# Half the memory tokens in activation places, the first key weight ahead of the memory, GDN ratios scaled on VectorE, and another order and other banks for the down projection

## The chip, the cores and the metric

The kernel runs on one core of a Trainium2 chip. The metric is the device time of one execution in microseconds; the profile that goes with it is one execution taken by the hardware profiler. A core has TensorE (matrix products, with a separate path for loading weights), VectorE, ScalarE, GpSimd and SyncE; each works through its own instructions in order, and waits on semaphores where it needs another engine's result. Transfers are issued on queues; this kernel issues nearly all of them from SyncE (SP), a few from ScalarE and VectorE.

## The reference

One layer of a hybrid encoder for 512 tokens of width 2048, with 256 memory tokens:

```python
h = x
y = rmsnorm(h, norm_mix) @ w_in                  # 7520 columns
h = h + concat[GDN(y_gdn), RWKV7(y_rwkv)] @ w_out
hn, mn = rmsnorm(h, norm_xattn), rmsnorm(mem, norm_mem)
q, k, v = hn @ wq, mn @ wk, mn @ wv              # 4 heads of 512
h = h + softmax(q k^T / sqrt(512)) v @ wo
hn = rmsnorm(h, norm_mlp)
h = h + square(relu(hn @ w_up)) @ w_down         # hidden 8192
out = rmsnorm(h, norm_final)
```

GDN is a gated delta rule with 8 heads of 128, RWKV7 a recurrence with 16 heads of 64. In chunks, both need the inverse of a unit lower triangular matrix for every head and chunk:

```python
M = where(strict, einsum(kb, kc) * gamma, 0)     # kb = k * beta, gamma = exp(G_i - G_j)
sol = triangular_solve(M + I, rhs)               # unit diagonal
```

All arithmetic is in 32 bits.

## The kernel before, in words

**Products.** A 32-bit operand is split into two parts of a reduced 32-bit type, `hi` (ScalarE copies it into that type) and `lo` (VectorE subtracts `hi` from the original). A product is then `hi hi + lo hi + hi lo`. For the 256 memory tokens a tile `mhl` of 512 columns holds `hi` in its left half and `lo` in its right, so one key weight block costs one product of 512 columns with the weight's `hi` and one of 256 with its `lo` (lines 594 to 603 of the listing below, in `projections`).

**Stages.** The program runs through these, with TensorE nearly always busy:

1. Input projection: 59 output blocks of 128 columns (`py0` to `py58`), each with a weight of 2048 x 128 in two halves of 512 KB. Meanwhile the heads of both recurrences are worked on as soon as their columns are there (`rwkv`, `gdn`); their small products stand between the large ones. The profile has the end of the last projection product at about 911 us.
2. Memory keys (`kp0` to `kp15`): 16 output blocks, each in two halves of 8 products with `hi` and 8 with `lo`. The first two blocks are worked on half by half: `kpo` gives (0,0), (1,0), (0,1), (1,1), then one block after the other. The last heads of the recurrences go on beside this.
3. Query weights times keys (`kq`), which starts only after the inverse of the last GDN head ("inverted", 7).
4. Attention, values and output, the recurrence's output product, written in plain order.
5. The MLP, up and then down, by a scheme of seven products on 2 x 2 blocks in place of eight: sums of blocks (`s1` to `s4` of the weights, `T1` to `T4` of the activations) are multiplied with each other, and every product is added to one or several output blocks. Names: `B11`, `B21`, `B22` are products of plain activation blocks, `T1` to `T4` those of sums. A unit is one (e, g) part of up or down; the units are a list, down has ten.

**What sets the order.** In stages 1 to 3, and again in stage 5, the program is written as generators (`chain(generator, rank)`) that yield one instruction at a time. A planner at build time (`run`, with `start`, `cost` and `issue`) keeps a clock for every engine and a landing time for every tile, and issues at each step the chain whose next instruction can start first; ranks break ties. A generator can also yield a condition (`after("x", 4)`, or a lambda), and is passed over until that holds. So the order on every engine follows from durations that the planner believes, and an edit in one chain moves instructions of others. A lane such as `SL` or `SM` is an engine or a queue with an extra wait or margin that the planner adds for its transfers.

**The weights' ring.** All weights of stages 1 to 3 come through a ring of raw tiles (`wraw`), in the order of the list `wq`; each entry is loaded when an earlier one has been split. Entries of kind "s" are memory tokens for the sum of squares, of kind "m" memory tokens for the keys (four k-blocks of 128 features each, 512 KB), of kind "w" weight halves. For "m", `memory` splits four k-blocks with the gain `norm_mem` into `mhl` tiles. These take the places of the activation tiles `xhi`, `xlo` of the projection, which share 32 buffers (tag "act"): `after("x", i)` holds when the last projection block `py58` is through with k-blocks up to i. The end of `wq` is: memory 0, 1, 2, first key weight half, memory 3, the other key weights.

**The inverses.** `inverse_blocks` writes the matrices to memory on SP, reads 16 x 16 diagonal blocks back in a layout for GpSimd, inverts them there, and writes and reads the result (tiles `bg..T`, `bg..U`); `inverse_levels` builds the 64 x 64 inverses from them on TensorE, with copies by VectorE. For GDN, the matrix is `NTm = pkk * Es`, with `pkk` the products of keys in the PSUM bank `pkk` and `Es = E * sneg`, E the ratios exp(G_i - G_j) and `sneg` the negative strict mask.

**Down's banks.** A unit of down works with three pairs of PSUM banks: `mm` for B21, `mg` for T1 and B22, and for the rest `scr` and `scg` in units of odd number, or two `mx` in units of even number (`odd` in `multiply_`). A product that adds to a bank which an earlier one of the same unit has used waits until VectorE has added that one into h ("snap" events, set in `downout`). The order of the seven products is given by `order_of`, with one order for the very last unit.

Nearly every instruction of stages 1 to 3 and 5 is issued at one line of `issue`, so the profile shows it as L256: the name of the tile tells what it is.

## Time and profile before

| what | us |
|---|---|
| median of 3 runs | 2902.29 |
| lowest and highest | 2901.53, 2903.21 |
| profiled execution | 2902.95 |
| its span, from first to last instruction | 2901.2 |

The profiled execution took 1.75 us more than its span. Its mean granted clock of TensorE is 0.999 of full speed.

A row of the timeline is a start in us, a length, the engine, the line of the kernel, the operation, output tile <- input tiles with partitions x elements, and the number of instructions joined in that row; in brackets stand the idle time before it on that engine and what ended it. PE is TensorE, PEld its weight load, DVE VectorE, ACT ScalarE, POOL GpSimd, SP SyncE; a q behind the name (SPq, ACTq) means the engine's queue of transfers, where a row's length is the issue's and not the transfer's. Buffer numbers are left out of names, so `kp` stands for all of `kp0` to `kp15`. Where several matrix products are joined, the last one's end includes its way through the array; the step between two is better read from the starts.

### The profile page before, as it was taken

How to read it: one execution, taken by the hardware profiler on the slowest of the kernel's cores; microseconds unless marked ns; L12 is line 12 of the kernel's file. 1: busy time of each engine (PE TensorE's matmuls, PEld its weight loads, DVE VectorE, ACT ScalarE, POOL GpSimd, SP SyncE). 2: the span in 40 equal slices, each digit the busy share in tenths (PEclk: the TensorE clock that was granted, in tenths of full speed). 3: DMA queues.
4: the chain of work that ended last, by engine and by line, in shares of the span. 5: the costliest groups of instructions: out<-in, count | busy, mean ns of one | idle time of the engine just before them, and what ended most of it. 6: DMA issues, size and time to landing. Idle time of an engine off the chain costs nothing.

```text
span 2901.2 us, 49161 instructions
## 1 busy us (share of the span) xinstructions
PE 2868.0 (99%) x18794; PEld 2420.4 (83%) x18794; DVE 2333.1 (80%) x3551; ACT 1569.9 (54%) x2233; POOL 227.0 (8%) x547
## 2 busy tenths in 40 slices
PE   8999999999999999999999999999999999999998
PEld 7877877777777888879988888888888888888887
DVE  7787787787887876769956898899998878787888
ACT  6454555545655555564444656555555645454544
POOL 0213213223122100000000000000000000000000
PEclk9999999999999999999999999999999999999999
DMA  5657556556656688684423344656665878978733
GB/s 190 175 143 184 160 160 173 161 154 185 173 154 198 199 256 276 229 286 159 125 94 94 106 157 158 196 194 203 187 201 181 291 243 278 296 256 273 267 102 109
DMA packets 320924, 553.01 MB, mean 191 GB/s; under 512 B 101096, under 2 KB 188396, under 8 KB 320688
## 3 DMA queue, kind: packets, MB, share of 16 engines
q1 hardware_dynamic: 293296, 518.41, 57.9%
q10 hardware_dynamic: 27392, 31.46, 3.1%
q8 instruction: 147, 2.41, 0.3%
q14 instruction: 89, 0.73, 0.1%
HBM read 443.45 MB, written 106.31 MB: 189 GB/s over the span
## 4 chain that ended last, share of the span: by engine, by line
PE 93%; DMA 2%; DVE 2%; ACT 1%; issue 1%; ACTq 0%; SPq 0%; DVEq 0%
PE py L256 22%; PE mxu L256 12%; PE mgd L256 6%; PE mgu L256 6%; PE mxd L256 6%; PE op L122 5%; PE vp L122 3%; PE mmu L256 3%; PE sc L122 3%; PE at L122 3%; PE mmd L256 3%; PE scrd L256 3%; PE scgd L256 3%; PE kq L256 3%; PE kp L256 3%; PE vo L122 1%
## 5 line engine op out<-in xcount | busy, mean ns | idle before, releaser
L256 ACT CAST whi<-wraw 128x1024 fp32r<-128x1024 f32 (+1 forms) x366 | 383.4, 1048 | 364.2 <-PE py L256 150.4
L256 DVE TENSOR_TENSOR wlo<-wraw,whi 128x1024 fp32r<-128x1024 f32 (+1 forms) x366 | 450.5, 1231 | 101.0 <-ACT whi L256 92.2
L256 PE MATMUL py<-xhi,whi 128*128 128x512 f32 x928 | 372.6, 401 | 8.1 <-ACT xhi L256 8.1
L256 PE MATMUL py<-xhi,wlo 128*128 128x512 f32 x928 | 372.8, 402 | 0.0
L256 PE MATMUL py<-xlo,whi 128*128 128x512 f32 x928 | 372.7, 402 | 0.0
L256 ACT CAST whi<-w 128x1024 fp32r<-128x1024 f32 x176 | 185.3, 1053 | 170.3 <-PE mxd L256 35.2
L256 DVE TENSOR_TENSOR wlo<-w,whi 128x1024 fp32r<-128x1024 f32 x176 | 214.8, 1221 | 44.4 <-ACT whi L256 41.1
L256 PE MATMUL mxu<-cb,whi 128*128 128x512 f32 x1016 | 249.3, 392 | 0.0
L256 PEld LDWEIGHTS mxu<-cb,whi 128*128 128x128 f32 x1016 | 184.7, 189 | 34.3
L256 PEld LDWEIGHTS py<-xhi,whi 128*128 128x128 f32 x928 | 175.0, 189 | 42.6 <-ACT xhi L256 8.1
L256 PEld LDWEIGHTS py<-xhi,wlo 128*128 128x128 f32 x928 | 175.0, 189 | 35.5 <-issue 1.8
L256 PEld LDWEIGHTS py<-xlo,whi 128*128 128x128 f32 x928 | 174.9, 189 | 34.8 <-DVE xlo L256 0.5
L131 DVE TENSOR_TENSOR wlo<-wraw,whi 128x1024 fp32r<-128x1024 f32 x112 | 136.6, 1221 | 44.0 <-ACT whi L130 43.5
L130 ACT CAST whi<-wraw 128x1024 fp32r<-128x1024 f32 x112 | 117.6, 1051 | 85.9 <-PE op L122 29.4
L256 PE MATMUL mxu<-cb,wlo 128*128 128x256 f32 x1016 | 142.7, 283 | 0.7 <-DVE wlo L256 0.7
L256 PEld LDWEIGHTS mxu<-cb,wlo 128*128 128x128 f32 x1016 | 135.1, 191 | 6.0 <-DVE wlo L256 0.9
L256 ACT ACT_TABLE_LOAD x87 | 111.6, 1283 | 36.4 <-DVE suml_gn L256 16.5
L256 PE MATMUL mgu<-cb,whi 128*128 128x512 f32 x512 | 129.3, 394 | 0.1
L256 PE MATMUL mxd<-whi,cb 128*128 128x512 f32 x512 | 126.7, 389 | 0.7 <-DVE acc L256 0.7
L256 PE MATMUL mgd<-whi,cb 128*128 128x512 f32 x512 | 126.4, 389 | 0.0
L256 ACT CAST whi<-ws 128x1024 fp32r<-128x1024 f32 x75 | 79.0, 1053 | 72.3 <-PE mgu L256 48.2
L122 PE MATMUL op<-ob,whi 128*128 128x256 f32 (+1 forms) x752 | 115.3, 304 | 0.1
(945 smaller groups left out, 6447.2 us busy)
## 6 DMA issues: line engine op xcount, KB each, us to landing
wraw<-in_w_in SPq DMA_DIRECT2D x116, 512.0 KB, 4.6
wraw<-in_w_up SPq DMA_DIRECT2D x65, 512.0 KB, 3.6
w<-in_w_up SPq DMA_DIRECT2D x63, 512.0 KB, 4.0
ds<-in_w_dm SPq DMA_DIRECT2D x128, 205.0 KB, 4.1
sd_s<-ds SPq DMA_DIRECT2D x128, 205.0 KB, 4.7
wraw<-sd_s SPq DMA_DIRECT2D x51, 512.0 KB, 4.9
w<-sd_s SPq DMA_DIRECT2D x50, 512.0 KB, 5.5
w<-in_w_dm SPq DMA_DIRECT2D x48, 512.0 KB, 5.0
```

Of the source, the lines that this page charges most:

```text
L122: PE.matmul(o, l, r, start=start, stop=stop, skip_group_check=again)
L130: S.copy(hi, src)
L131: V.tensor_tensor(out=lo, in0=src, in1=hi.bitcast(F32), op=ALU.subtract)
L256: f(*a, **k)
```

## The change

It has four parts.

1. In `wq` the first key weight half stands ahead of the memory entries, and only memory 0 and 1 come through the ring. Memory 2 and 3 are loaded by a new chain, `straight`, in four transfers of 256 KB on SP (lane `SD`: no extra wait, a landing margin of 1500 ns), directly into four of the 32 activation places. For this the 32 buffers are divided into 28 with tag "act" and 4 with tag "acr": `act_tile` puts `xhi4`, `xlo4`, `xhi5`, `xlo5` into the four (`x in (4, 5)`), and afterwards the tiles that come to those places by count. The first two of these loads wait for `after("x", 4)`, the others for `after("x", 5)`. A second new chain, `placed`, splits `mhl8` to `mhl15` from there, after `mhl7` has been begun; `mhl` is a dictionary now.
2. In `gdn` the multiplication `E * sneg` moves from GpSimd, ahead of the key's norm, to VectorE, directly ahead of the multiplication with `pkk`. It occurs once for each of 8 heads.
3. The last unit of down takes T1 second, B22 ahead of T3: B11, T1, T2, B22, T3, B21, T4.
4. `odd` is turned round: in all ten units of down the banks `scr`, `scg` and the two `mx` are exchanged, so the first unit of down uses `scr` and `scg`, the last one `mx`.

Since the planner orders stages 1 to 3 anew, part 1 and 2 move instructions beyond their own. The new lane takes a line above `issue`, so the issue line reads L257 in the changed kernel.

SP's queue around the last RWKV inverse, in the kernel before. `sr<-ndri7` above the first row is the read for GpSimd, `bg16T` and `bg16U` write the inverted blocks, `r` and `E2` read them, `wraw<-in_wk` is a key weight half, `wraw<-in_memT` memory tokens, `ds` and `sd` belong to sums of down's weights that are worked out early.

```order
L256 DMA bg16T_195<-sr_549_10077 64x16x16
L256 DMA bg16U_196<-sr_549_10077 64x16x16
...
L256 DMA r_557_10299<-bg16T_195 64x8x64 x2
L256 DMA E2_558_10300<-bg16U_196 64x4x64 x4
L256 DMA wraw126_10395<-in_wk 128x1024
L256 DMA sd3_1_s1_154<-ds02_55_829 128x410
L256 DMA sd3_1_s3_156<-ds01_54_828 128x410
L256 DMA wraw127_10444<-in_memT 128x1024
L256 DMA sd3_1_s2_155<-ds00_53_827 128x410
L256 DMA wraw128_10475<-in_wk 128x1024
```

And in the changed kernel, first at the read for the inverse, then from `bg16T` on (`mraw` are the four new loads):

```order
L257 DMA sr_549_10099<-ndri7_10094 64x16x16
L257 DMA wraw123_10126<-in_wk 128x1024
L257 DMA wraw124_10175<-in_memT 128x1024
...
L257 DMA bg16T_195<-sr_549_10099 64x16x16
L257 DMA bg16U_196<-sr_549_10099 64x16x16
L257 DMA wraw125_10354<-in_memT 128x1024
L257 DMA r_563_10357<-bg16T_195 64x8x64 x2
L257 DMA E2_564_10358<-bg16U_196 64x4x64 x4
L257 DMA mraw0_10417<-in_memT 128x512
L257 DMA mraw1_10425<-in_memT 128x512
L257 DMA mraw2_10428<-in_memT 128x512
L257 DMA mraw3_10434<-in_memT 128x512
L257 DMA wraw126_10402<-in_wk 128x1024
```

The first key weight (`wraw126` before, `wraw123` now) moved from behind the eight transfers of the inverse to the place right after its read; the second (`wraw128` before, `wraw126` now) stands behind the four `mraw`.

TensorE at the end of the key products, before: `gi7u` is the last product of the last GDN inverse, `TtG` the copy of it by VectorE, `gs2_7_0` the first product that reads that copy.

```order
L256 MATMUL kp13_11636<-mhl15_10571,whi_144_11602 128x512
L256 MATMUL gi7u1_11609<-TtG_194,gkn_591_11560 64x64 x4
L256 MATMUL kp14_11700<-mhl0_10364,whi_145_11638 128x512
L256 MATMUL kp14_11700<-mhl1_10376,whi_145_11638 128x512
...
L256 MATMUL kp14_11700<-mhl7_10439,whi_145_11638 128x512
L256 MATMUL gs2_7_0_11729<-gv_587_11324,TtG_194 128x128
L256 MATMUL kp14_11700<-mhl0_10364,wlo_145_11639 128x256
```

And in the changed kernel:

```order
L257 MATMUL kp15_11762<-mhl14_10572,whi_148_11728 128x512
L257 MATMUL kp15_11762<-mhl15_10620,whi_148_11728 128x512
L257 MATMUL gi7u1_11734<-TtG_194,gkn_591_11682 64x64 x4
L257 MATMUL gs2_7_0_11841<-gv_587_11554,TtG_194 128x128
L257 MATMUL kq0_0_0_11843<-khl0_10660,whi_149_11764 128x512
L257 MATMUL kq0_0_0_11843<-khl1_10715,whi_149_11764 128x512
L257 MATMUL kq0_0_0_11843<-khl2_10849,whi_149_11764 128x512
```

The key products that stood behind `gi7u` stand ahead of it now; `gs2_7_0` follows on `gi7u` directly, and the first query product `kq0` after that.

TensorE in the last unit of down, before: the end of B11 (`wlo_261`) and the start of T2 (`whi_262`). `scr` and `scg` are the banks, `cb` the activations.

```order
L256 MATMUL scgd3_1_0_1_27235<-whi_261_17933,cb0_7_17866 128x512
L256 MATMUL scrd3_1_0_0_27234<-wlo_261_17934,cb0_6_17150 128x512 x2
L256 MATMUL scgd3_1_0_1_27235<-wlo_261_17934,cb0_6_17150 128x512 x2
L256 MATMUL scrd3_1_0_0_27234<-whi_262_17935,cb0_2_17146 128x512
L256 MATMUL scrd3_1_0_0_27234<-whi_262_17935,cb0_3_17147 128x512
```

And in the changed kernel, the end of B11 and the start of what follows it, T1:

```order
L257 MATMUL mxd3_1_0_1_27239<-whi_261_17949,cb0_7_17882 128x512
L257 MATMUL mxd3_1_0_0_27238<-wlo_261_17950,cb0_6_17166 128x512 x2
L257 MATMUL mxd3_1_0_1_27239<-wlo_261_17950,cb0_6_17166 128x512 x2
L257 MATMUL mgd3_1_1_0_27272<-whi_262_17951,cb5_6_17201 128x512
L257 MATMUL mgd3_1_1_0_27272<-whi_262_17951,cb5_7_17887 128x512
```

B11 now fills the `mx` banks, and the product behind it goes to `mg` instead of to the banks that B11 has just filled.

The diff, without its unchanged surroundings where these tell nothing:

```diff
...
                 return self.key, nm, getattr(self.eng, nm), a, k, out, aps, self.slack
             return op
 
+    SD = Lane(nc.sync, "SP", 0.0, 1500.0)
     SL, SM = Lane(nc.sync, "SP", wait=6000.0), Lane(nc.sync, "SP", margin=8000.0)
     DV, AC, GS, TE, SY = (Lane(e, k) for e, k in ((V, "DVE"), (S, "ACT"), (GP, "POOL"), (PE, "PE"), (nc.sync, "SP")))
 
...
         yield TE.matmul(pt, which, hi, start=False, stop=True)
         lock.pop()
 
-    def act_tile(nm, dt=F32R):
-        return tile_of(pa, [P, 512], dt, "act", nm, 32)
+    acts = [0]
+
+    def act_tile(nm, dt=F32R, x=None):
+        few = x in (4, 5)
+        if x is None:
+            few = acts[0] // 4 in (7, 11, 19, 27, 35)
+            acts[0] += 1
+        return tile_of(pa, [P, 512], dt, "acr" if few else "act", nm, 4 if few else 28)
 
     mixd = [pd.tile([P, T], F32, name=f"mixd{i}", tag=f"mixd{i}") for i in range(16)]
     KQd = [pd.tile([P, 1024], F32, name=f"kqd{i}", tag=f"kqd{i}") for i in range(16)]
...
                 yield from presum(e, m, c, min(c + width, 2048), d, Lane(nc.sync, "SP", margin=5000.0), Lane(nc.sync, "SP", 0.0, 0.0))
 
     hk = [("w", I["wk"][n][:, h * 1024:(h + 1) * 1024]) for n, h in kpo]
-    wq += [("m", m) for m in mem4[:3]] + hk[:1] + [("m", mem4[3])] + hk[1:]
+    wq += hk[:1] + [("m", m) for m in mem4[:2]] + hk[1:]
     wq += [("w", I["wqT"][n][:, g * 1024:(g + 1) * 1024]) for n in range(KD) for g in range(2)]
     NKP, NKQ = 2 * NIN, 2 * NIN + 2 * KD
     raws, halves, used, whole, piece = {}, {}, set(), set(), {}
...
                 whole.add(w)
                 w += 1
             else:
-                yield from (memory if kind == "m" else squares)(nm % 4, raws[i])
+                yield from (memory if nm >= 4 else squares)(nm % 4, raws[i])
                 nm += 1
             if NWR < i + NWR <= 2 * NWR:
                 chain(late(i + NWR), 2)
...
 
     def xin():
         for k in range(KD):
-            hi, lo = act_tile(f"xhi{k}"), act_tile(f"xlo{k}")
+            hi, lo = act_tile(f"xhi{k}", x=k), act_tile(f"xlo{k}", x=k)
             yield from split_(xr[k], hi, lo, col("norm_mix", k))
             xhi.append(hi)
             xlo.append(lo)
...
             wh, wl = halves[NKP + i]
             for part in (0, 1) if h == 0 else (1, 0):
                 for k in range(8 * h, 8 * h + 8):
-                    yield lambda: len(mhl) > k
+                    yield lambda: k in mhl
                     if part == 0:
                         yield TE.matmul(pt, wh[:, k % 8 * P:k % 8 * P + P], mhl[k], start=k == 0, stop=k == KD - 1)
                     else:
...
             yield DV.scalar_tensor_tensor(out=E[:, cs], in0=E[:, cs], scalar=RT[:, c, 0, h:h + 1],
                                           in1=K("mbias"), op0=ALU.subtract, op1=ALU.min)
         yield AC.activation(E, E, AF.Exp)
-        Es = tl("gEs")
-        yield GS.tensor_tensor(out=c3(Es), in0=c3(E), in1=K("sneg").unsqueeze(1).broadcast_to([P, 4, P]), op=ALU.mult)
         kn = yield from normed(k_, None, "gkn", 0)
         kb = tl("gk")
         yield DV.tensor_tensor(out=kb, in0=kn, in1=B, op=ALU.mult)
...
         for c in range(4):
             cs = slice(c * P, (c + 1) * P)
             yield TE.matmul(pkk[:, cs], kn[:, cs], kb[:, cs], start=True, stop=True)
-        NTm = Es
-        yield DV.tensor_tensor(out=NTm, in0=pkk, in1=Es, op=ALU.mult)
+        NTm = tl("gEs")
+        yield DV.tensor_tensor(out=c3(NTm), in0=c3(E), in1=K("sneg").unsqueeze(1).broadcast_to([P, 4, P]), op=ALU.mult)
+        yield DV.tensor_tensor(out=NTm, in0=pkk, in1=NTm, op=ALU.mult)
 
         def store(full):
             yield SY.dma_start(full[:, 0:4, :], c3(NTm)[hA, :, 0:64])
...
             chain(gdn(h + 1), 3)
 
 
-    mhl = []
+    mhl, direct = {}, {}
     mrs = rstd[:, 0:M]
     macc = []
 
...
             k = 4 * k4 + i
             yield after("x", k // 2)
             t = act_tile(f"mhl{k}")
+            if k == 7:
+                events.add(("direct",))
             yield from split_(raw[:, i * M:(i + 1) * M], t[:, 0:M], t[:, M:2 * M], col("norm_mem", k))
-            mhl.append(t)
+            mhl[k] = t
+
+    def straight():
+        for j in range(4):
+            yield after("x", 4 + j // 2)
+            t = tile_of(pa, [P, 512], F32, "acr", f"mraw{j}", 4)
+            yield SD.dma_start(t.rearrange("p (a b) -> p a b", b=M), mem4[2 + j // 2][:, j % 2 * 2:j % 2 * 2 + 2, :])
+            direct[j] = t
+
+    def placed():
+        yield after("direct")
+        for k in range(8, KD):
+            yield lambda: (k - 8) // 2 in direct and ("x", k // 2 + 2) in events
+            t, raw = act_tile(f"mhl{k}"), direct[(k - 8) // 2][:, k % 2 * M:k % 2 * M + M]
+            yield from split_(raw, t[:, 0:M], t[:, M:2 * M], col("norm_mem", k))
+            mhl[k] = t
 
     def memnorm(pt, mw):
         yield from rsq_(mw, pt[:, 0:M], 1.0 / 2048, b_eps6)
...
     chain(pieces(), 1)
     chain(consts(), 3)
     chain(loader(), 2)
+    chain(straight(), 1)
+    chain(placed(), 2)
     chain(xin(), 1)
     chain(xsum(), 4, ("rstd",))
     chain(derived(), 3, ("derived",))
...
         if u[0] == "u":
             return (B11, A11), (T1, "s1"), (T2, "s2"), (B21, A12), (T3, "s3"), (B22, "s4"), (T4, A22)
         if u == units[-1]:
-            return (B11, A11), (T2, "s2"), (T1, "s1"), (T3, "s3"), (B22, "s4"), (B21, A12), (T4, A22)
+            return (B11, A11), (T1, "s1"), (T2, "s2"), (B22, "s4"), (T3, "s3"), (B21, A12), (T4, A22)
         return (B11, A11), (B21, A12), (T2, "s2"), (T1, "s1"), (T3, "s3"), (B22, "s4"), (T4, A22)
 
     left = {}
...
         for u in units:
             kind, e, g = u[:3]
             if kind == "d":
-                odd = units.index(u) % 2
+                odd = units.index(u) % 2 == 0
                 tags = {B21: ("mm", "mm"), T1: ("mg", "mg"), B22: ("mg", "mg")}
                 for i, w in order_of(u):
                     tag = tags.get(i, ("scr", "scg") if odd else ("mx", "mx"))
```

## The prediction

> **What bounds the kernel now.** I read the page first, then who waits for whom on TensorE, then a table of windows by stage, then the instructions in time around the four places that the change touches.
>
> ```profile
> span 2901.2 us, 49161 instructions
> PE 2868.0 (99%) x18794; PEld 2420.4 (83%) x18794; DVE 2333.1 (80%) x3551; ACT 1569.9 (54%) x2233; POOL 227.0 (8%) x547
> ...
> PE py L256 <- ACT xhi L256: 8.1, 1, 8.1
> PE kp L256 <- ACT whi L256: 4.4, 1, 4.4
> ...
> 20.00:900.00 880.00, 877.44 (x7791) 701.70 (x7790) 680.69 (x1247) 477.86 (x669) 203.85 (x495) 1.00 0.59 166
> 911.00:920.00 9.00, 4.62 (x42) 3.04 (x42) 2.89 (x5) 5.20 (x9) 0.00 (x0) 0.81 0.89 287
> 920.00:940.00 20.00, 17.92 (x294) 15.36 (x293) 16.76 (x28) 11.37 (x19) 1.54 (x6) 1.00 0.68 211
> 960.00:1045.00 85.00, 84.42 (x635) 72.91 (x635) 68.94 (x127) 45.06 (x71) 0.00 (x0) 1.00 0.68 212
> ```
>
> In the wait rows the numbers are total, times, longest; in the window rows length, then busy time of PE, PEld, DVE, ACT, POOL, then the granted clock. TensorE is busy in 2868.0 of 2901.2 us, so nothing that only shortens another engine's work is worth anything. What can be won is TensorE's 33.2 us of idle time, and time at a lower clock. 8.1 of it is the start, which the change leaves alone. The largest wait after that is the 4.4 us ahead of `kp`, the first product of the memory keys. Between 20 and 900 us, the whole input projection, only 2.56 us are idle.
>
> The profiled run took 2902.95 us, 1.75 more than its span; the median of the runs is 2902.29. I work in span differences and take them from the median, since 0.66 us is far below what I can forecast. About 0.2%, 5.8 us, is what a measurement of this kernel can tell from no change.
>
> **Part 1: the memory tokens and the first key weight.** These rows, picked from the timeline by time, show the stall and the prices around it (start, length, engine, operation; idle before and its releaser in brackets):
>
> ```profile
> 902.12 0.58 SPq L256 DMA_DIRECT2D bg16T<-sr  x1
> 907.02 2.61 SPq L256 DMA_DIRECT2D E<-bg16U  x4
> 909.73 0.55 SPq L256 DMA_DIRECT2D wraw<-in_wk  x1
> 914.75 1.04 ACT L256 CAST whi<-wraw 128x1024 fp32r<-128x1024 f32 x1 [5.80 <-DMA wraw<-in_wk]
> 915.85 2.58 PE L256 MATMUL kp<-mhl,whi 128*128 128x512 f32 x6 [4.38 <-ACT whi L256]
> 925.79 2.08 PE L256 MATMUL kp<-mhl,whi 128*128 128x512 f32 x8
> 901.14 2.04 DVE L256 SCALAR_TENSOR_TENSOR mhl<-wraw,prm,mhl 128x256 fp32r<-128x256 f32 x4
> 919.52 0.42 DVE L256 TENSOR_TENSOR k<-ri7x,cst 128x256 f32<-128x256 f32 x1 [1.98 <-PE ri7w L256]
> 936.37 3.82 PE L256 MATMUL kp<-mhl,whi 128*128 128x512 f32 x16
> 940.02 2.08 PE L256 MATMUL kp<-mhl,wlo 128*128 128x256 f32 x16
> ```
>
> The first key weight is issued at 909.73, behind the inverse's eight transfers on SP, and lands 5.0 us later; TensorE had run out of work at 911.5. The cost is more than the 4.38 us: afterwards six key products take 2.58 us, while eight take 2.08 us at 925.79. The window 911 to 920 has a mean clock of 0.81, so 0.19 x 9 = 1.7 us more went there, and the window 920 to 940 holds 20 - 17.92 = 2.1 us of waits of the last recurrence head. Together 4.4 + 1.7 + 2.1 = 8.2 us.
>
> After the change the weight's load stands 14 instructions ahead of the inverse's `bg16T` instead of 6 behind it, so it is converted before the projection ends, and the 4.4 and the 1.7 have no cause left in it. What is late next is the second key weight: on SP it now stands behind the four new 256 KB loads, which follow the same eight transfers (2.61 us for the four of `E` alone). Those four also wait until TensorE is done with its tiles 4 and 5, 7.5 us before the projection's end, so this wait is over when the inverse's transfers are.
>
> Walk, with E = 911.3 as the end of the last projection product. TensorE does four key products and the 0.9 us of `ri7x` (from 918.4, the end of the six, to about 919.3, just ahead of VectorE's reading it), then the other 12 of the first half: it wants the second weight at about E + 3.7 = 915.0. If the inverse ends when it did (902.1), SP comes to the four loads at 909.1 and to that weight at 10.8 us past 900; with the 5.0 us to land and 1.04 to convert it is there at 916.6, 1.6 us late. On VectorE it is followed by four memory splits (2.04 us) and two 0.42 us results of `ri7x`, which hold up the next inverse product by 2.2 us. TensorE is then through `pkk` at 927.9, where before it was at 925.8, but with 33 more key products done, half of them at (940.02 - 936.37)/16 = 0.228 us and half, the narrow ones, at 2.08/16 = 0.13, 5.8 us: gain 3.7. If the inverse ends 3.5 us earlier, the weight is there in time and only 0.8 us of the second wait is left: gain 6.7. Why it may:
>
> ```profile
> 878.15 0.59 SPq L256 DMA_DIRECT2D ndri<-GB  x1
> 878.83 2.03 SPq L256 DMA_DIRECT2D ds<-in_w_dm  x4
> 881.90 0.60 SPq L256 DMA_DIRECT2D sr<-ndri  x1
> sr<-ndri SPq DMA_DIRECT2D x1, 64.0 KB, 6.3
> ```
>
> The read that starts the inverse takes 6.3 us to land behind four weight pieces, an output and a 512 KB load; one piece is left ahead of it in the new order, and its small neighbours land in 2.5 to 2.9. I take the middle, **-5.2 us** (ends -3.7 and -6.7). Every split and transfer is counted in it: 16 splits as before, two 512 KB loads fewer, four of 256 KB more.
>
> **Part 2: the scaled ratios on VectorE.** Eight multiplications leave GpSimd and join VectorE, each with the form of the second row:
>
> ```profile
> 904.80 1.44 POOL L256 TENSOR_TENSOR gEs<-gE,cst 128x512 f32<-128x512 f32 x1 [1.91 <-ACT gE L256]
> 930.01 0.68 DVE L256 TENSOR_TENSOR gEs<-pkk,gEs 128x512 f32<-128x512 f32 x1
> ```
>
> 8 x 0.68 = 5.4 us of VectorE work in a stage where VectorE is busy 680.69 of 880 us and TensorE idles 2.56. Cover: the projection's own products, always there to be issued; without it each head would lose up to 0.68 us. I take **0**, ends -1 and +1.5. GpSimd is at 8%; nobody waits for its release.
>
> **Part 3: the end of the key products.** The reorder puts 64 more matrix rows ahead of the last GDN inverse, so that the keys are used up just when `gi7u` comes:
>
> ```profile
> 1017.11 0.68 PE L256 MATMUL gi7u<-TtG,gkn 64*64 64x64 f32 x8
> 1018.48 0.41 DVE L256 COPY TtG<-gi7u 64x256 f32<-64x256 f32 x1
> 1019.67 0.38 PE L256 MATMUL gs<-gv,TtG 128*128 128x128 f32 x2
> 1029.77 0.49 PE L256 MATMUL gs<-gEs,gkt 128*128 128x128 f32 x2 [0.58 <-DVE gEs L256]
> ```
>
> Before, eight key products lay between `gi7u` and `gs`, which covered the 0.41 us copy. Now nothing does: copy plus hand-overs, about 0.9 us. Further on, three products (0.7 us, or 0.4 for narrow ones) cover several such copies; the one wait shown, 0.58, had three as well. The window 960 to 1045 already holds 0.58 of idle time. **+1.2 us**, between +0.3 (the copy runs at once, the rest hidden) and +2.5 (four more waits of 0.4).
>
> **Part 4: down's banks and last unit.**
>
> ```profile
> 2280.05 1.07 PE L256 MATMUL mxd<-whi,cb 128*128 128x512 f32 x4
> 2281.84 1.20 PE L256 MATMUL mxd<-whi,cb 128*128 128x512 f32 x4 [0.72 <-DVE acc L256]
> 2857.28 0.61 PE L256 MATMUL scgd<-wlo,cb 128*128 128x512 f32 x2
> 2858.85 1.16 PE L256 MATMUL scrd<-whi,cb 128*128 128x512 f32 x4 [0.96 <-DVE h L256]
> 2858.62 0.68 DVE L256 TENSOR_TENSOR h<-h,scgd 128x512 f32<-128x512 f32 x1
> 2891.13 0.61 PE L256 MATMUL scgd<-wlo,cb 128*128 128x512 f32 x2
> 2896.59 0.34 ACTq L256 DMA_DIRECT2D out_dram<-h  x1
> ```
>
> Down's first unit waits for an `mx` bank that up's last product still fills. Four products at 0.228 us step 0.91; here the step is 1.79, so 0.9 us is lost. With `scr`/`scg`, idle since the transposes, the wait has no cause: **-0.9** (0 if the next weight half is late instead; the halves stand about 2 us ahead there). In the last unit the second product reuses B11's banks while VectorE still adds them into h: 2858.85 instead of 2857.28 + 0.45 = 2857.73, 1.1 us. In the new order T1 comes between, in banks `mg`; its second half of weights is split after the two additions, by about 2860.5, and TensorE needs it at 2862.3. Every later product that reuses a bank now has another between. **-1.1** (end -0.2 if that split comes a microsecond late). The tail from TensorE's last issue at 2891.13 to the last store at 2896.59 has the same operations in nearly the same order: 0, ends -0.3 and +0.3.
>
> **Sum.** -5.2 + 0 + 1.2 - 0.9 - 1.1 = -6.0; 2902.3 - 6.0 = **2896.3 us** (0.9979). The rest of the recurrence's order changes too: 11 switches fewer between projection and recurrence products, 16 more among shapes. No row prices a switch by itself; I take 0 and leave 1.5 us either way in the range.
>
> **A rule beside the row.** The 4.38 us wait was followed by a clock of 0.81, and the 0.72 and 0.96 us waits of part 4 were not followed by anything like it. The Trainium skill, TensorE: Matmul & The Clock Gate, section "Part 1: The HAM clock gate", says that the array falls to half rate after an idle window of about 3.4 us and returns after as long a busy one. The trace agrees. By that rule the remaining waits of part 1, 2.2 us at most, cost nothing at the clock and the 1.7 us goes whole, as the sum has it; if the clock lost in proportion to waiting, 1.7/4.38 of up to 3.8 us would come back and the sum would be -4.5.
>
> **Rivals.**
> - *The boundary is covered entirely and the GDN tail costs nothing.* For it: the early inverse above. Then -6.7 - 0.9 - 1.1 - 0.8 of the later waits = -9.5, 2892.8 us. Against it: three short covers in part 3. Chance 0.20.
> - *The stall only moves.* The second weight and the splits behind the new loads cost what the first did: DMA engines are busy at 0.89 from 911 to 920, so landing may take 6 us and more. Then part 1 gives -1.5, and -1.5 + 1.2 - 2.0 = -2.3, 2900.0 us. Against it: the first weight gives 2.8 us of cover that wasn't there. Chance 0.20.
> - *Slower: the last GDN inverse comes too late for the query products.* Its start needs `pkk`'s result, which VectorE now takes after two more splits, and its transfers sit on SP:
>
> ```profile
> 956.36 0.62 POOL L256 COPY sgi<-sgi 32x256 f32<-32x256 f32 x1
> 970.18 0.42 SPq L256 DMA_DIRECT2D bg8T<-sgi  x1
> 976.38 2.52 SPq L256 DMA_DIRECT2D gqn<-bg8U  x4
> 996.94 0.27 PE L256 MATMUL gi7x<-gk,gEs 64*64 64x64 f32 x2
> ```
>
>   It was ready at about 981.5 and used at 996.9, 15 us of slack, which SP's 13 us hold after 957 has eaten into. Past these 15 us each microsecond is TensorE's, since no key products are left; slower by 0.2% needs 27 us. At that, 2908.5 us. Chance 0.05.
>
> The forecast case has 0.55, and as it lies on the bound, 0.32 of it counts as faster by over 0.2% and 0.23 as within. With the rivals: **faster 0.52, within 0.2% 0.43, slower 0.05**. The range reaches over the first two rivals: 2892.3 to 2901.0. Its own range for the forecast case, from the ends of part 1 and 3, is 2894 to 2899.
>
> **What would show it.** Right: no wait of over 3 us ahead of `kp`, a clock of 1.00 from 911 to 920, under 5 us lost there; no wait at the first `scrd` of down or in the last unit; `gs` waiting about 1 us in all just after `kq` begins; VectorE 3 to 6 us busier. Wrong: a `kp` wait on `whi` some 3 us into the key products, a clock under 1, waits for `gn`, `pkk` or `gi` between 20 and 900 us beyond 4 us, or a longer tail after the last product. A time outside the range would mean that the recurrence's new order, not these four places, decides.

## The result and the profile after

| what | before | after |
|---|---|---|
| median, us | 2901.46 (13 runs) | 2894.96 (13 runs) |
| lowest and highest | 2899.65, 2903.61 | 2893.59, 2897.72 |
| ratio, 95% interval | | 0.9979 (0.9972 to 0.9986) |
| span of the profiled execution | 2901.2 | 2891.8 |

The change makes the kernel 6.5 us faster; 2896.3 and a ratio of 0.9979 were forecast. The profiled execution of the changed kernel is the fastest of its 13 and lies 9.4 us under the profiled one of before, some 3 us more than the medians differ, so below a stage is only called changed where several profiles agree. Three of TensorE's waits in the kernel before, and then the page of the changed kernel with its longest waits but that of the start (total, times, longest):

```profile
PE gn L256 <- DVE suml_gn L256: 2.6, 4, 0.7
PE scrd L256 <- DVE h L256: 1.0, 1, 1.0
PE mxd L256 <- DVE acc L256: 0.7, 1, 0.7
...
span 2891.8 us, 49180 instructions
PE 2864.7 (99%) x18794; PEld 2421.4 (84%) x18794; DVE 2333.4 (81%) x3559; ACT 1573.5 (54%) x2233; POOL 219.3 (8%) x539
...
PE kp L257 <- DVE wlo L257: 1.9, 1, 1.9
PE kp L257 <- ACT whi L257: 1.8, 1, 1.8
PE gs L257 <- DVE TtG L257: 1.2, 1, 1.2
```

The 4.4 us ahead of `kp` is gone, and so are the four waits of `gn` (2.6 us), which no term of the sum covers, down's `mxd` and the last unit's `scrd`. In their place stand two waits on key weights and one of `gs`. Around the start of the keys the timeline reads:

```profile
895.28 0.58 SPq L257 DMA_DIRECT2D bg16T<-sr  x1
901.77 2.03 SPq L257 DMA_DIRECT2D mraw<-in_memT  x4
903.89 0.38 SPq L257 DMA_DIRECT2D wraw<-in_wk  x1
906.19 1.07 PE L257 MATMUL kp<-mhl,whi 128*128 128x512 f32 x4
910.69 1.04 ACT L257 CAST whi<-wraw 128x1024 fp32r<-128x1024 f32 x1 [4.52 <-DMA wraw<-in_wk]
911.79 2.74 PE L257 MATMUL kp<-mhl,whi 128*128 128x512 f32 x8 [1.83 <-ACT whi L257]
991.21 1.79 PE L257 MATMUL kp<-mhl,wlo 128*128 128x256 f32 x8 [1.86 <-DVE wlo L257]
1023.98 0.49 PE L257 MATMUL gs<-gv,TtG 128*128 128x128 f32 x2 [1.16 <-DVE TtG L257]
```

The first key product comes at 906.19, directly behind the last projection product. The second weight is issued at 903.89 behind the four loads of memory tokens and lands 6.8 us later. But the projection itself is also shorter, with the same number of TensorE's instructions ahead of the first `kp` (7882): from its first product to its last 898.1 us pass here, and 897.3 and 900.4 in two more profiles of the changed kernel, against 902.5 before and 903.0 and 903.1 in two kernels that keep the old place of part 2's multiplication (`down_only` and `memory_order`); of the kernels with the new place only `weight_first` takes as long, 903.3. No term of the sum had that.

### The profile page after: what moved, and what is told of

It is laid out like the page before. It is cut to its first block, busy times and chain, and to the rows that moved or that the text cites. A ratio compares the mean times of both kernels' runs of the same rounds, so it can differ in the third digit from the quotient of the medians.

```text
span 2891.8 us, 49180 instructions
## 1 busy us (share of the span) xinstructions
PE 2864.7 (99%) x18794; PEld 2421.4 (84%) x18794; DVE 2333.4 (81%) x3559; ACT 1573.5 (54%) x2233; POOL 219.3 (8%) x539
## 4 chain that ended last, share of the span: by engine, by line
PE 93%; DMA 3%; DVE 2%; ACT 1%; issue 0%; ACTq 0%; SPq 0%; DVEq 0%
PE py L257 22%; PE mxu L257 12%; PE mgd L257 6%; PE mgu L257 6%; PE mxd L257 6%; PE op L122 5%; PE vp L122 3%; PE mmu L257 3%; PE sc L122 3%; PE at L122 3%; PE scrd L257 3%; PE scgd L257 3%; PE mmd L257 3%; PE kp L257 3%; PE kq L257 3%; DMA wraw<-in_wo 1%
## 5 line engine op out<-in xcount | busy, mean ns | idle before, releaser
L257 ACT CAST whi<-wraw 128x1024 fp32r<-128x1024 f32 (+1 forms) x365 | 382.8, 1049 | 372.4 <-PE py L257 137.6
L257 DVE TENSOR_TENSOR wlo<-wraw,whi 128x1024 fp32r<-128x1024 f32 (+1 forms) x365 | 446.0, 1223 | 89.7 <-ACT whi L257 81.1
L257 PE MATMUL py<-xhi,whi 128*128 128x512 f32 x928 | 373.4, 402 | 7.8 <-ACT xhi L257 7.8
L257 PE MATMUL py<-xhi,wlo 128*128 128x512 f32 x928 | 372.8, 402 | 0.0
L257 PE MATMUL py<-xlo,whi 128*128 128x512 f32 x928 | 372.1, 401 | 0.0
L257 ACT CAST whi<-w 128x1024 fp32r<-128x1024 f32 x178 | 187.6, 1054 | 173.9 <-PE scgd L257 44.0
L257 DVE TENSOR_TENSOR wlo<-w,whi 128x1024 fp32r<-128x1024 f32 x178 | 217.4, 1222 | 43.4 <-ACT whi L257 40.8
L257 PE MATMUL mxu<-cb,whi 128*128 128x512 f32 x1016 | 249.3, 392 | 0.0
L257 PEld LDWEIGHTS mxu<-cb,whi 128*128 128x128 f32 x1016 | 184.7, 189 | 34.3
L257 PEld LDWEIGHTS py<-xhi,whi 128*128 128x128 f32 x928 | 175.2, 189 | 42.9 <-ACT xhi L257 7.8
L257 PEld LDWEIGHTS py<-xhi,wlo 128*128 128x128 f32 x928 | 175.1, 189 | 34.5 <-issue 1.0
L257 PEld LDWEIGHTS py<-xlo,whi 128*128 128x128 f32 x928 | 175.1, 189 | 33.7 <-DVE xlo L257 0.5
L257 PE MATMUL mxu<-cb,wlo 128*128 128x256 f32 x1016 | 142.7, 283 | 0.7 <-DVE wlo L257 0.7
L257 PEld LDWEIGHTS mxu<-cb,wlo 128*128 128x128 f32 x1016 | 135.1, 191 | 6.0 <-DVE wlo L257 0.9
L257 PE MATMUL mgu<-cb,whi 128*128 128x512 f32 x512 | 129.4, 394 | 0.1
L257 PE MATMUL mxd<-whi,cb 128*128 128x512 f32 x512 | 126.8, 389 | 0.0
L257 PE MATMUL mgd<-whi,cb 128*128 128x512 f32 x512 | 126.4, 389 | 0.0
L257 ACT CAST whi<-ws 128x1024 fp32r<-128x1024 f32 x75 | 78.9, 1052 | 64.1 <-PE mgu L257 48.1
```

Of the source, the lines that this page charges most:

```text
L257: f(*a, **k)
```

## The experiments

Gains are against the kernel before in the same series (2900.7 to 2901.8 us). "vp" is the time of the first value product in the profile, where all that parts 1 and 2 touch is over (1126.3 us before, 1119.7 after).

**1. Ratios and banks alone; memory and last unit alone.** Both start from the kernel before. `ratio_banks` has part 2 as in the change's diff and part 4; `memory_order` has part 1 as in that diff and part 3:

```diff
 ratio_banks
-                odd = units.index(u) % 2
+                odd = units.index(u) % 2 == 0
 memory_order
-            return (B11, A11), (T2, "s2"), (T1, "s1"), (T3, "s3"), (B22, "s4"), (B21, A12), (T4, A22)
+            return (B11, A11), (T1, "s1"), (T2, "s2"), (B22, "s4"), (T3, "s3"), (B21, A12), (T4, A22)
```

> The kernel before with parts 2 and 4 alone: the scaled ratios on VectorE, and down's banks exchanged (the order of the last unit as before). Theory: the 5 us by which the changed kernel's projection ends sooner come from the ratios, whose move changes the order of the GDN heads' products. Then the last projection product ends at 906 us, give or take 1, instead of 911.3, the four waits of gn (2.6 us) are gone, the wait of about 4.4 us ahead of kp and a half clock behind it stay, down's first unit has no wait (1.0 us less), the last unit keeps its 1.0. In all 5 to 6 us less than before. Rival: the gain ahead of the keys comes with the new places of the memory tokens. Then the projection ends at 911, and the kernel is 1 us faster than before.

> The kernel before with parts 1 and 3 alone: the memory tokens and the first key weight, and the new order of the last unit (ratios on GpSimd, banks as before). Theory: the projection ends at 911 as before; the wait ahead of kp goes, but the second key weight is 1 to 2 us late and brings its own stretch of half clock, so that the keys begin only 1 to 3 us better; the last unit has no wait (1.2 less) and the tail behind the last product is 0.8 longer. In all 1.5 to 3.5 us less than before. Rival: part 1 carries nearly all of the change's gain, then the projection ends at 906 and the kernel is 5 to 6 us faster than before.

Measured: `ratio_banks` 2894.91 us, ratio 0.9980 (0.9971 to 0.9989), vp at 1120.2; `memory_order` 2905.41 us, ratio 1.0017 (1.0008 to 1.0026), vp at 1127.4. So the ratios and the banks alone bring the whole gain, and the memory tokens, with part 3 beside them, make the kernel slower. In `ratio_banks` the inverse and the first key weight are early although the order of the loads is the old one. The wait of 4.4 us ahead of `kp`, which the theory let stand together with its half clock, is gone; two shorter ones for key weights (0.84 and 1.65 us) and one of 1.5 us for the inverse stand in its place, and the clock stays at full speed:

```profile
896.78 0.58 SPq L256 DMA_DIRECT2D bg16T<-sr  x1
903.27 0.60 SPq L256 DMA_DIRECT2D wraw<-in_wk  x1
...
PE kp L256 <- ACT whi L256: 2.5, 2, 1.6
```

The inverse's write came at 902.12 before. In `memory_order` it comes at 902.34, as late as ever; the four memory loads are then issued between its reads and land late, and TensorE waits for their splits, first 1.76 and then 5.88 us:

```profile
908.60 1.97 SPq L257 DMA_DIRECT2D mraw<-in_memT  x4
910.62 1.24 SPq L257 DMA_DIRECT2D E<-bg16U  x2
924.58 0.98 PE L257 MATMUL kp<-mhl,wlo 128*128 128x256 f32 x2 [1.76 <-ACT mhl L257]
931.44 0.98 PE L257 MATMUL kp<-mhl,wlo 128*128 128x256 f32 x2 [5.88 <-ACT mhl L257]
```

For `memory_order` both the theory and the rival had part 1 gaining something. It does not, without part 2.

**2. Is it the engine or the place?** Part 2 changes both: the multiplication goes to VectorE, and behind the key products. `pool_late` changes the place alone, `vector_early` the engine alone:

```diff
 pool_late
-        Es = tl("gEs")
-        yield GS.tensor_tensor(out=c3(Es), ...)
         kn = yield from normed(k_, None, "gkn", 0)
...
+        NTm = tl("gEs")
+        yield GS.tensor_tensor(out=c3(NTm), ...)
 vector_early
-        yield GS.tensor_tensor(out=c3(Es), ...)
+        yield DV.tensor_tensor(out=c3(Es), ...)
```

> The kernel before, with the multiplication by the mask left on GpSimd, but put at the new place, behind the key products. Its order on TensorE and on SP around the last RWKV inverse is that of the kernel with the ratios on VectorE: the products pgA and pgB stand in 16 unbroken groups instead of 23, the read of the inverse stands ahead of three of the four weight pieces. Theory: the gain of part 2 is this order, not the engine or the 0.68 us: no waits of gn, the projection ends at 906 to 908, the wait ahead of kp is under 2 us with no half clock behind it, 4.5 to 6 us less than before (2895 to 2896.5). Rival: it is VectorE's shorter multiplication; then with GpSimd's 1.44 us ahead of the store of each GDN inverse the time stays within 1.5 us of before's 2901.

> The kernel before, with the multiplication by the mask on VectorE at its old place, ahead of the key's norm. The order has 16 groups of pgA and pgB, one of them behind another product, and the read of the last RWKV inverse stands ahead of all four weight pieces, but the first key weight stays behind the eight transfers. Theory (the order): about as pool_late, 4 to 6 us less than before. Rival (the new place behind the key products is what helps, since the norm of the keys no longer waits for VectorE or GpSimd): at most 2 us less, with the waits of gn still there.

Measured: `pool_late` 2892.07 us, ratio 0.9969 (0.9957 to 0.9981), 9 us faster than before with none of the other parts in, and 3 us more than the theory had; vp at 1115.6. `vector_early` 2932.03 us, ratio 1.0109 (1.0095 to 1.0123), 31 us slower, where theory and rival both had a gain. So the new place brings the gain and VectorE is not needed for it; at the old place VectorE costs 31 us. In neither kernel does TensorE wait for the multiplication itself. What differs is the order that the planner makes of everything else once this instruction stands elsewhere. That this order is the cause, and not the place as such, is read from the traces: no run moves the instruction and keeps the rest of the order. `vector_early` shows how far an order reaches: in its profile 14 us are lost by vp, and 12 in down, where its longest wait stands. Its largest waits of TensorE, and two rows from VectorE and TensorE:

```profile
PE mxd L256 <- ACT whi L256: 9.4, 1, 9.4
PE rs L256 <- DVE BK L256: 8.7, 3, 5.6
PE kp L256 <- ACT whi L256: 7.8, 2, 6.3
...
277.27 0.58 DVE L256 TENSOR_TENSOR ds<-ds,ds 128x410 f32<-128x410 f32 x1 [6.68 <-DMA ds<-in_w_dm]
278.04 0.69 PE L256 MATMUL rs<-BK,BTz 128*128 128x64 f32 x2 [5.58 <-DVE BK L256]
```

Here a sum of down's weights (`ds`), work that nobody is in a hurry for, stands on VectorE ahead of a result that TensorE needs, and its transfer has not landed: 6.68 us for VectorE, 5.58 for TensorE.

What the good order does better could be read in the traces of the kernels with the new place (these three effects were not separated by runs). First, the inverse: its read is issued at 875 to 879 (881.90 before; `weight_first`, below, is an exception with 881.15), with one weight piece between its writes and itself (before: four pieces, an output and a 512 KB load) and GpSimd starts 3 us behind it instead of 6.4. The first row is the kernel before, the other two are `pool_late`:

```profile
888.33 0.38 POOL L256 TENSOR_TENSOR sr<-sr 64x15 f32<-64x15 f32 x1 [25.27 <-DMA sr<-ndri]
...
877.09 0.59 SPq L256 DMA_DIRECT2D sr<-ndri  x1
879.99 0.21 POOL L256 TENSOR_TENSOR sr<-sr 64x15 f32<-64x15 f32 x1 [23.30 <-DMA sr<-ndri]
```

Second, `gn`: at most two waits of 1.2 us together in place of four. Third, unbroken groups: the 128 pairs `pgB`, `pgA` of the RWKV heads have matrices of 64 rows. With the new place they stand in 16 groups of eight pairs, before in 23 groups between other products. The price is in the trace of before:

```profile
320.12 0.39 PE L256 MATMUL py<-xhi,wlo 128*128 128x512 f32 x1
320.44 0.37 PE L256 MATMUL pgB<-AR,BK 64*128 64x128 f32 x1
320.66 0.27 PE L256 MATMUL pgB<-AR,BK 64*128 64x128 f32 x1
320.77 0.27 PE L256 MATMUL pgB<-AR,BK 64*128 64x128 f32 x1
...
322.19 0.27 PE L256 MATMUL pgB<-AR,BK 64*128 64x128 f32 x1
322.39 0.50 PE L256 MATMUL py<-xhi,whi 128*128 128x512 f32 x1
322.73 0.40 PE L256 MATMUL py<-xlo,whi 128*128 128x512 f32 x1
```

Into the group a step is 0.32 instead of 0.23, the first pair 0.22 instead of 0.11, out of it 0.20 instead of 0.11, the next large product 0.34 instead of 0.23: about 0.4 us for every group that is broken off. The Trainium skill, TensorEngine Tiling (Array Packing), section "Key Properties", says that a change of tiling mode drains TensorE; the trace agrees and adds this price. But other groups are broken off more often in the new order. Counted over all products of fewer than 128 rows, 147 groups became only 144 between the first and the last projection product, and the steps into, inside and out of them add up to 170.0 us before and to 167.7 to 168.6 with the new place: about 2 us, not 7 times 0.4. And these three effects do not make an order good by themselves: `vector_early` has the 16 groups, no wait of `gn` and a GpSimd that starts 3 us behind the read, which itself comes 16 us later than before, and loses 31 us by waits elsewhere.

**3. Part 1 beside the good order.** `no_memory` is the changed kernel without part 1. `late_down` is `pool_late` with parts 3 and 4, `late_all` that with part 1 as well (the changed kernel with `GS` for `DV` in the moved line).

```diff
 no_memory, against the changed kernel
-    wq += hk[:1] + [("m", m) for m in mem4[:2]] + hk[1:]
+    wq += [("m", m) for m in mem4[:3]] + hk[:1] + [("m", mem4[3])] + hk[1:]
...
-    chain(straight(), 1)
-    chain(placed(), 2)
```

> The changed kernel without part 1: memory tokens and first key weight as before, the other three parts in. Theory: with the inverse early by part 2, the first key weight comes in time even behind the eight transfers, so part 1 is worth little: 2893 to 2895.5, at most 1.5 us more than the changed kernel; several waits of 0.8 to 1.7 us at the start of the keys, none of which fills half of a 3.4 us stretch, so no half clock. Rival (part 1 as I forecast it): it brings 3.7 us or more, so this kernel takes 2897 or more, with a wait of over 3 us ahead of kp.

> The run pool_late (the multiplication by the mask on GpSimd, but behind the key products) with parts 3 and 4 added; the memory tokens as before. Theory: the places are what part 2 gained by, and down's two edits add 1.0 + 1.2 - 0.8 = 1.4 us to pool_late's gain of 8.8: 10 us less than before, 2890.5 us, and 3 us less than the changed kernel in this series. Rival: pool_late's lead over the kernels with the ratios on VectorE was chance; then it stands level with the changed kernel, 2892.5 to 2895.

> The changed kernel with the multiplication on GpSimd at the new place, so late_down with part 1 added. Theory: with the inverse early, part 1 brings nothing; the second key weight, behind four loads of memory tokens, leaves a wait of 1.8 to 2.7 us and a half clock behind it where that fills half a stretch: 0 to 4 us more than late_down. Rival (my forecast of part 1): 3.7 us less than late_down or more.

Measured: `no_memory` 2893.43 us, ratio 0.9974 (0.9965 to 0.9984), vp at 1120.9. The changed kernel had ratios of 0.9979, 0.9972 and 0.9982 in its three series. `late_down` 2892.18 us, 0.9964 (0.9951 to 0.9976); `late_all` 2892.62 us, 0.9965 (0.9952 to 0.9979). Part 1 is worth nothing that can be measured in either pair; without it, no wait near the keys is longer than 1.5 us. In `late_all` the second weight is only 0.6 us late, less than I expected. `late_down` stands 4 us below the changed kernel of its own series (2896.26, next item), with intervals that barely overlap, and beats the kernel before by 9.6 us. From `no_memory` only the engine of the multiplication sets it apart; GpSimd is the better by 0.0010 in the ratio, which lies within the intervals. `late_all` and the changed kernel of the same series are a pair of this kind too: GpSimd is the better by 3.6 us, again with intervals that overlap. With `pool_late` and `ratio_banks`, three pairs point the same way. So the move to VectorE, half of part 2, brought nothing and probably cost a few us, which no single pair shows.

**4. The changed kernel again, twice.**

> The changed kernel itself once more, to see which of its differences come again. Theory: all waits of over 1 us stand at the same places with the same lengths to within 0.2 us, and where TensorE waits for more than about half of one of the 3.4 us stretches in which the clock is granted, the next stretch is at half; the wait of 1.8 us may or may not bring that, by where it falls. The 1.7 us that the changed kernel gained between the first value product and the output product, where nothing was changed, is chance and does not all come again. Rival: that gain is the change's (transfers or buffers that lie differently) and comes again in full. Time 2895, give or take 2.

> The changed kernel for comparison in the same series: 2892.5 to 2895.5 us, a wait of about 2 us some 5 us into the keys with a half clock of 3.4 us behind it.

Measured: 2892.59 us (0.9972, 0.9961 to 0.9983) and 2896.26 us (0.9982, 0.9973 to 0.9991), each less than 1 us outside what I expected of it; vp at 1117.0 and 1120.7. The wait for the second key weight comes again (2.1 and 1.8 us), each time with a stretch of half clock; that of `gs` too (1.2 and 1.2). The wait near 990 us is 0.75 and 1.6 us instead of 1.86, so "to within 0.2 us" was too strict. From vp to the first output product 178.6 us pass before, and 176.9, 177.0 and 177.3 in the changed kernel's three profiles, but also 176.5 in `down_only` below, where all that is ahead stands as before, and 179.4 in `late_all`, which has the change's parts 1, 3 and 4 and the new place: so that gain does not go with parts 1 and 2, and I take it for chance.

**5. The second key weight first.**

```diff
-    chain(straight(), 1)
+    chain(straight(), 4)
```

> The changed kernel with one rank changed, which puts the second key weight (and three small transfers behind it) ahead of the four loads of memory tokens on SP. Theory: the second weight was late because it stood behind these four, so the wait of 1.8 us some 4 us into the keys goes, and with it the half clock of 3.4 us that follows it: 3 to 3.5 us less than the changed kernel, 2891.5 us. Rival: the DMA engines are busy at 0.97 and over there, so whatever stands first, the same bytes have to land; then a split of memory tokens is late instead, a wait of 1 to 3 us on mhl takes the place of the one on whi, and the time stays within 1 us of the changed kernel's.

Measured: 2891.89 us, 0.9969 (0.9957 to 0.9980), 0.7 us under `after_again` of the same series, whose interval covers it. The wait for the weight is gone; a wait for the last RWKV inverse stands in its place, since the memory splits that VectorE takes ahead of that inverse's results now come late (three of them, from 915.14 on):

```profile
916.65 0.42 DVE L257 TENSOR_TENSOR k<-ri7x,cst 128x256 f32<-128x256 f32 x1
...
PE ri7s L257 <- DVE k L257: 2.6, 1, 2.6
```

The time is the rival's, and so is the kind of wait, though the rival expected it at `mhl`: what stands first is taken from what stands next.

**6. Down alone, and another order of the last unit.** `down_only` is the kernel before with parts 3 and 4. `unit_order` is the changed kernel with B21 and B22 exchanged in its last unit:

```diff
-            return (B11, A11), (T1, "s1"), (T2, "s2"), (B22, "s4"), (T3, "s3"), (B21, A12), (T4, A22)
+            return (B11, A11), (T1, "s1"), (T2, "s2"), (B21, A12), (T3, "s3"), (B22, "s4"), (T4, A22)
```

> The kernel before with parts 3 and 4 alone. Everything up to down stands in the same order as before, so the projection and the keys show the old waits (4.4 us ahead of kp, the half clock). My forecast: down's first unit 0.9 less, the last unit 1.1 less, the tail unchanged (9.8 us from the last product to the end): 2.0 us less than before. Rival, from the changed kernel's trace: 1.0 and 1.2 less, but the tail 0.8 longer, 1.4 us less. In time 2899 to 2900; only the trace tells the two apart.

> The changed kernel with the last unit in the order B11, T1, T2, B21, T3, B22, T4. Theory: the tail behind the last product grew by 0.8 us in the changed kernel because T3, whose results are scaled and squared for the output, came later, next to T4; here it comes at the same distance from the end, but B22 and not B21 stands last but one, so the tail is between 9.8 and 10.6 us and there is still no wait in the last unit: 0 to 0.8 us less than the changed kernel. Rival: the tail depends on T4 alone (10.6 as in the changed kernel).

Measured: `down_only` 2899.42 us, 0.9994 (0.9985 to 1.0002), no difference that can be told. Its trace shows the waits ahead of the keys as before (4.6 us ahead of `kp`), none in down, and a tail of 10.5 us, as the rival had it. `unit_order` 2895.61 us, 0.9985 (0.9976 to 0.9994): no wait in the unit, but from the start of the last product to the end 13.5 us pass. Against the theory the tail does not shrink, and against the rival it does not depend on T4 alone: with B22 last but one the output rows become complete later, and their scaling and stores pile up behind the last product. In the changed order the tail is longer by less (the first row is the kernel before):

```profile
2891.78 0.69 DVE L256 TENSOR_TENSOR h<-h,scgd 128x512 f32<-128x512 f32 x1 [0.58 <-PE scgd L256]
...
2880.48 0.68 DVE L257 TENSOR_TENSOR h<-h,h 128x512 f32<-128x512 f32 x1
2881.00 0.61 PE L257 MATMUL mxd<-wlo,cb 128*128 128x512 f32 x2
2882.47 0.68 DVE L257 TENSOR_TENSOR h<-h,mxd 128x512 f32<-128x512 f32 x1
```

The last result is taken 1.47 us behind the issue of its products (before: 2891.78 - 2891.13 = 0.65), because VectorE got a multiplication by the final gain at 2880.48 and, behind it, two scalings that had been done earlier before. From the start of the last product to the end it is 10.5 to 10.6 us in all nine profiles with the changed kernel's order, and 9.8 in all four with the old.

## Why the number was right and its reasons mostly not

The forecast of -6.0 us lies 0.5 from the measured -6.5. By its own steps:

- **Part 1, -5.2: wrong.** Alone (with part 3, -0.4) it is some 5 us slower, beside part 2 it is worth nothing. The step that failed is "Why it may": I saw that the inverse's read would land sooner in the new order and booked that under the memory tokens, though the walk's bad end ("if the inverse ends when it did") is what part 1 alone would have met, and even that end was too kind. The earlier inverse comes with part 2. The walk's second weight is 1.6 us late (1.8 by its own figures, 910.8 + 5.0 + 1.04 = 916.8 against 915.0), and 1.83 in the changed kernel's trace, but that is luck too: SP came to this weight 2.3 us ahead of the projection's end and not 0.5, and the weight took 6.8 us to land and not 5.0.
- **Part 2, 0: wrong, and the whole gain.** `ratio_banks` gains 5.8 us, 1.0 of it by the banks. I priced the instruction (0.68 us forecast, 0.69 measured) and not the new order that it makes the planner write; the projection that came out shorter is no term of the sum. It is the new place that gains, 9 us in `pool_late`, and not the engine. VectorE's total of busy time did not rise by 5.4 us either (2333.1 before, 2333.4 after).
- **"No row prices a switch": wrong.** The rows under experiment 2 were in the trace of before, at 0.4 us a group, and all such steps together became some 2 us less. The counts were of no help: in the traces the switches between projection products and others rise from 633 to 643, where the prediction has 11 fewer.
- **The clock: wrong.** By the rule of the Trainium skill as I applied it, I held that waits of at most 2.2 us cost nothing at the clock. But waits of 1.83 and 1.86 us were each followed by a half clock of 3.41 us, up to 1.7 us of lost work, as much as the wait of 4.38 had cost. Nor does the trace of before agree as far as the prediction says: of the stretches ahead of that half clock none was idle as a whole (88% the one, 41% the other; rows in the last section).
- **Part 3's place, +1.2: right in kind.** `gs` waits 1.16 us right behind `gi7u` in all five profiles with the changed kernel's order there, where before one of 0.58 stood; the further waits that I allowed for did not come.
- **Down, -0.9 and -1.1: right.** From its first product to the end of its first quarter, down takes 1.0 us less, and the last 160 products 1.2 less (37.25 us before, 36.04 after). **The tail, 0: missed by 0.7 to 0.8**, since the multiplication by the final gain moved closer to the end than "nearly the same order" allowed.
- **The rivals.** "The stall only moves" described part 1 best. The slower one, the last GDN inverse, did not come to pass.
- **The signs.** Right ones came (no wait over 3 us ahead of `kp`, none at down's first `scrd` or in the last unit, `gs` at 1.16 us), but so did three of the wrong ones: a `kp` wait on `whi` some 4 us into the keys, a half clock from 913.09 to 916.50, and a longer tail. By its own signs the prediction was not right, whatever its number.

So two errors of about 5 us with opposite signs cancelled, by luck. The test that told them apart was to run each part alone; the sum could not have.

## What to carry to other kernels

Where a planner writes the order, an edit's first price is the new order, on every engine, and not the edited instruction: compare both orders for broken groups, for waits whose releaser moves, and for what stands ahead of each read on the transfer queue. Then move the instruction without changing its engine, and change its engine without moving it, before believing in either. A forecast that comes out right is no evidence for its terms until each part has been run alone.

## What the runs showed of the hardware that I had not expected

TensorE's clock is granted in stretches of 3.41 us, and in these traces a stretch at full clock in which TensorE idles for about half is followed, nearly always, by one at half rate. The rows give a stretch's length, then busy time of PE, PEld, DVE, ACT, POOL, then the granted clock (and the DMA engines' share and GB/s). The first two are the kernel before, the next pair is the changed kernel, the next three rows `weight_first` (two waits of 1.07 and 1.02 us, most of which fell into one stretch), then `ratio_banks`, `after_third`, and `late_all` at its last products:

```profile
909.44:912.85 3.41, 2.02 (x9) 1.32 (x7) 1.65 (x3) 0.00 (x0) 0.00 (x0) 1.00 0.64 149
912.85:916.26 3.41, 0.41 (x2) 0.38 (x3) 0.44 (x1) 1.49 (x3) 0.00 (x0) 1.00 1.01 341
...
909.67:913.09 3.42, 1.58 (x9) 1.14 (x8) 1.32 (x2) 2.40 (x5) 0.00 (x0) 1.00 1.10 265
913.09:916.50 3.41, 3.19 (x47) 2.46 (x47) 2.15 (x6) 1.60 (x4) 0.00 (x0) 0.50 0.86 317
...
816.09:819.50 3.41, 1.68 (x10) 0.94 (x8) 3.38 (x8) 0.00 (x0) 2.05 (x4) 1.00 0.74 176
819.50:822.91 3.41, 3.05 (x9) 2.67 (x10) 2.11 (x8) 0.00 (x0) 0.00 (x0) 0.50 0.55 143
822.91:826.33 3.42, 3.42 (x12) 2.77 (x10) 2.27 (x5) 1.04 (x1) 0.00 (x0) 0.50 0.25 53
...
911.58:914.99 3.41, 1.86 (x50) 1.52 (x50) 2.94 (x7) 1.47 (x4) 0.00 (x0) 1.00 0.95 240
914.99:918.41 3.42, 1.90 (x36) 1.64 (x32) 0.00 (x0) 0.97 (x1) 0.00 (x0) 1.00 1.02 390
...
990.31:993.72 3.41, 1.84 (x13) 1.56 (x12) 2.44 (x5) 2.93 (x4) 0.00 (x0) 1.00 0.82 311
993.72:997.14 3.42, 3.42 (x20) 2.97 (x19) 2.80 (x3) 1.43 (x2) 0.00 (x0) 1.00 0.70 208
...
2879.09:2882.50 3.41, 1.53 (x7) 0.94 (x5) 3.09 (x7) 1.63 (x5) 0.00 (x0) 1.00 0.76 229
2882.50:2885.91 3.41, 0.00 (x0) 0.00 (x0) 2.62 (x6) 2.21 (x6) 0.00 (x0) 1.00 1.04 364
```

TensorE busy for 1.58 or 1.68 of 3.41 us (idle for 54 and 51%) brings a half clock; busy for 1.84 to 1.90 (idle for 46% at most) does not. Of the fourteen profiles two stand against a border between these. In `late_all` the stretch with the last products, idle for 55%, was followed by a full clock. In `vector_early` one stretch at 608.8 us, idle for only 36% but filled with products of 64 rows among others, was followed by a half clock. The way back does not follow idle time either: the half clock of `weight_first` went on for a second stretch behind one that idled for only 10%, while that of `unit_order` ended behind one that idled for 16% (busy 2.85 of 3.41 us from 911.59). So idle time is a good guide here, but may not be exactly what counts. It may also tell a part of the spread between executions: by this border a wait of 1.8 us would bring a half stretch or not, by whether it falls within one stretch or across two; no two runs here show the same wait both ways. The Trainium skill, TensorE: Matmul & The Clock Gate, section "Part 1: The HAM clock gate", has the length of the window (3413 ns) and that it runs freely, and the traces agree; that a whole idle window is needed, as I read it, they do not bear out.
